# A ninth full set of block products in place of a half-depth one, plain merge gates, first block loads that the scheduler may place, and five background turns per tile of the first branch

## The chip, the cores and the metric

The kernel runs on one core of one Trainium2 chip. The metric is the device time of one execution in microseconds (us). Of the kernel before, three runs gave 1087.9, 1088.07 and 1090.32 us; the median is 1088.07. TensorE is called PE in the profile, VectorE DVE, ScalarE ACT, GpSimd POOL, SyncE SP; PEld is TensorE's loading of stationary operands.

## What is computed

One decoder layer in float32, for 256 tokens of width 2048:

```python
h = rmsnorm(x, pre_norm_g)
(a_q, a_k, a_v, a_g, a_lr, b_q, b_k, b_v, b_g, m_a, m_b) = split(h @ w_in)
o_a = rmsnorm(gla_chunked(a_q, a_k, a_v, gk(a_lr))) * silu(a_g)      # 4 heads
o_b = rmsnorm(diff_attention(b_q, b_k, b_v)) * (1 - lam_init) * silu(b_g)  # 16 heads
merged = sigmoid(m_a) * (o_a @ w_branch_a) + sigmoid(m_b) * (o_b @ w_branch_b)
out = x + rmsnorm(merged @ w_out, post_norm_g)
```

`w_in` has 2048 rows and some 18,000 columns; the other three matrices are 2048 by 2048. Nearly all the work is these products. `a_g`, the gate of the GLA branch (gated linear attention), and `m_a`, the merge gate of that branch, have 2048 columns each, which the kernel handles in four groups of 512: `ag0` to `ag3` and `m00` to `m03`.

## The kernel before, in words

**Precision.** Each float32 weight tile is split into a high part `hi` (ACT, line 362) and a rest `lo` (DVE, line 363), both in the fast format fp32r, and the activations are kept in two parts as well. A product takes three matmuls (hi by hi, hi by lo, lo by hi). The unit of the program is a *half tile*: 128 by 1024 weights, one `hi`, one `lo`. `take` hands out half tiles in the order of one list, `seq`, and prepares three of them ahead; `load` (L313) brings weights on SP's queue when a staging buffer is free.

**Plain tiles** (`token_major`). Both blocks of 128 tokens against 512 columns: eight half tiles of 12 matmuls, each 512 columns wide. **Channel tiles** (`half_channel`): 16 matmuls per half tile, the weights stationary, the result transposed.

**Sets** (`block_products`). A full set treats tokens, depth and 1024 weight columns as a 2 by 2 matrix of blocks and computes it with seven block products instead of eight, in the order `PRODUCTS`. A product has four half tiles (`t` and `h` are 0 or 1) of 6 matmuls each, so a set has 28 half tiles and 168 matmuls where two plain tiles have 16 and 192. The sums of weight blocks which the method needs are made by accumulating DMAs on POOL's queue (L256) and by DVE (L265), eight of these per set. Before, there are eight full sets (0 to 7) and a ninth, "quarter" one (`SETS` = 8) of half the depth: `ag3` and `m02` over half of the 2048 rows, 14 half tiles. The remaining halves of those two are plain tiles of four half tiles each (`QUARTER`); their sums with the quarter set's results are made by DVE on `rest` tiles fetched from DRAM. `ag0` and `ag1` are set 7; `ag2` is a plain tile of eight half tiles.

**Order in the set phase.** `phase_steps` writes it out: behind certain half products (`PARTNERED`) stands one half tile of other work, a *partner* (the last value group `v4`, the GLA keys and queries, the first two groups of differential queries and keys), 72 in all. A set takes eight, except at two slots named in `ALONE`; the first two products of set 0 take one more per slot (`front`).

**Behind the sets.** `ag2`, `ag3`, `m02`, then the query and key tiles of head groups 2 and 3, then `m03`; then the first branch, `y00` to `y03` (L1340 and on; of `y03` four half tiles), then the second branch and the output product. Beside them run background tasks, generators that do one step whenever a tile calls `pump`: first the scores of GLA (`gla_scores`, `pool.memset(suf)` on L960), then `gla_out`, which waits for four gates and so for `ag3`, and two lanes of differential attention (`diff_lane`). Behind `m03` the program pumps without other work until `gla_out` is done. In a plain tile `pump` is called after half tiles 1, 3, 5 and 7, otherwise `pump_eager`, which steps a task only if it said "go". A step of a lane: `scores` (matmuls L1134 to L1140, maxima on DVE, exponentials on ACT), `combine` (DVE, L1160), `turned` (three transposes on PE, L1165), `weighted` (L1176 to L1178; squares on ACT, a root on POOL, L465, then DVE, L1188), and per pair of heads `turned_out` (four transposes, L1194).

**Queues.** PE, ACT, DVE, POOL and SP each work through their instructions in the order that a scheduler has fixed; `keep_in_program_order` pins an instruction to its place in the program. DMAs of SP and POOL are issued by these two in that order too.

Of the kernel before, what the change touches and what calls it, by code (L numbers as in the profile page):

```python
# [14 lines left out]
P = 128  # L15
# [9 lines left out]
LANES = 3  # L25
X_LOADS = {0: (2, 2), 1: (4, 4), 2: (8, 4), 3: (12, 4)}
# [3 lines left out]
SETS = 8  # L30
GLA_GATES = 7
QUARTER = ("ag3", "m02")
MERGE = (0, 1, 6)
LEAD = 6
EARLY = (0, 1)
PARTNERED = ((1, 1), (3, 1), (5, 1), (6, 0), (6, 1), (2, 1), (7, 0), (7, 1))
SPILL_AT = (6, 0, 0)
LAST_PARTNERED = (1, 3, 5, 6, 2, 7)
ALONE = ((2, 6, 1), (5, 6, 1))
# [15 lines left out]
def chunk_plan():  # L55
# [16 lines left out]
    plan.append((f"set{GLA_GATES}", "set", "w_in", [(4096, 1024)]))  # L72
    plan.append((f"set{SETS}", "quarter", "w_in", [(5632, 512), (o + 9216, 512)]))
    for g in range(4):
        if g > 1:
            plan.append((f"ag{g}", "rest" if g == 3 else "tok", "w_in", [(4096 + 512 * g, 512)]))
# [3 lines left out]
        if g > 1:  # L80
            plan.append((f"m0{g}", "rest" if g == 2 else "tok", "w_in", [(o + 8192 + 512 * g, 512)]))
# [10 lines left out]
def tiles_of(n, kind):  # L92
# [3 lines left out]
    if kind == "quarter":  # L96
        return [(8 * i, 4, 512 * j, 512) for i in range(2) for j in range(2)]
    if kind == "rest":
        return [(r, 4, 0, n) for r in (4, 12)]
# [7 lines left out]
def phase_steps():  # L107

    keys = ["v4"] + [f"{name}{hf}{c}" for hf in range(2) for name in ("k", "q") for c in range(4)]
    keys += [f"{name}{g}{c}" for g in EARLY for pair in range(2) for name in ("dq", "dk") for c in (2 * pair, 2 * pair + 1)]  # L110
    other = [(key, r, h) for key in keys for r in range(4 if key == "v4" else 1) for h in range(2)]
    slots = [(s, prod, t) for s in range(SETS) for prod in PRODUCTS for t in range(2)]
    slots += [(SETS, prod, 0) for prod in PRODUCTS]
    front = [(0, prod, t) for prod in PRODUCTS[:2] for t in range(2)]
    mixed = []
    for slot in slots:
        mixed += [("set", *slot, h) for h in range(2)]
        s, prod, t = slot
        with_partner = prod in LAST_PARTNERED if s == SETS else (prod, t) in PARTNERED and slot not in ALONE
        for _ in range(with_partner + (slot in front)):  # L120
            mixed.append(other.pop(0))
# [29 lines left out]
def hybrid_kernel(ctx: ExitStack, tc, xt, xn, preg, postg, w, w2, gkb, glag, lamv, diffg, ident_d, causal_d, lmask_d, out):  # L151
# [60 lines left out]
    def heads_order(g):  # L212
        return halves_of(*(f"{name}{g}{c}" for pair in range(2) for name in ("dq", "dk") for c in (2 * pair, 2 * pair + 1)))

    seq = halves_of("v0", "v2", "v3") + phase_steps()
    seq += halves_of("ag2", "ag3", "m02") + heads_order(2) + heads_order(3) + halves_of("m03", *(f"y0{g}" for g in range(4)))[:-4]
# [10 lines left out]
    def block(s, i, t):  # L227
        return weights(f"set{s}", i if s == SETS else 2 * i + t)[0]

    def link(s, name, t):  # L230
        count[0] += 1
        c = blocks.tile([P, 2048], F32, tag="chain", name=f"{name}_{count[0]}", bufs=5)
        tc.keep_in_program_order((pool if s else sp).dma_start(c, block(s, {"a": 0, "b": 3}[name], t)))
        chain[s, name, t] = c

    def emit_set(s, prod, t, h):
        c = slice(1024 * h, 1024 * h + 1024)
        few = 1 if s == SETS else 2
        name, i = {(2, 0): ("a", 0), (7, 1): ("a", 1), (4, 0): ("b", 0), (4, 1): ("b", 1)}.get((prod, t), (None, 0))
        if h == 0 and s < SETS and name and (i == 0 or s + 1 < SETS):  # L240
            link(s + 1, name, i)
        if h == 0 and s == 0 and prod == 1:
            link(s, "b", t)
        n = 2 * few * (PRODUCTS.index(prod) - PRODUCTS.index(2)) + 2 * t + h + LEAD
        if 0 <= n < 2 * few:
# [6 lines left out]
    def follow_set(s, prod, t, h):  # L252
# [7 lines left out]
        steps = {(5, 0): 0, (2, 0): 0} if s == SETS else {(5, 1): 0, (6, 0): 1, (2, 1): 0, (7, 0): 1}  # L260
        i = steps.get((prod, t))
# [501 lines left out]
    gspill = [None] * (2 * SETS + 2)  # L763

    def merge_gate(banks, parts=None):
        t = u2([P, 2, 512], "mgate")
        for b in range(2):
            src = banks[b]
            if parts:
                src = parts[b]  # L770
                dve.tensor_tensor(out=src, in0=banks[b], in1=src, op=ALU.subtract)
            act.activation(t[:, b, :], src, AF.Tanh, scale=half_rstd[:, b : b + 1])
# [14 lines left out]
    def others():  # L787
# [24 lines left out]
        for g in EARLY:  # L812
# [879 lines left out]
```

## Time and profile before

| | |
|---|---|
| runs of the kernel before | 1087.9, 1088.07, 1090.32 us |
| the profiled execution's own time | 1087.73 us |
| its span in the profile | 1086.0 us |
| busy: PE, DVE, ACT, POOL | 1075.1, 939.7, 742.1, 164.0 us |
| matmuls recorded | 5416 |
| moved by DMA | 292.40 MB |

The span lies 1.73 us below the profiled execution's own time, and that lies 0.34 us below the median. A row of a timeline gives start, length, engine, line, operation, output and inputs, with the engine's idle time before it and who ended that in brackets; a length contains the pipeline, so the pace of PE is read from one start to the next. In a table by windows stands, per stretch, the busy time of each engine with its number of instructions, then PE's granted clock, the busy share of the DMA engines and GB/s.

### The profile page before, as it was taken

The page shows a single profiled execution, that of the slowest core. Times are in us where ns is not written, and L with a number is a line of the kernel's source. Part 1 is how long each engine was busy: PE and PEld are TensorE (multiplying, and loading weights), DVE is VectorE, ACT ScalarE, POOL GpSimd, SP SyncE. Part 2 cuts the span into 40 slices and gives each one's busy share as a digit, 9 for nine tenths or more (in the row PEclk, how much of TensorE's full clock was granted, in tenths as well). Part 3 has the DMA queues.
Part 4 walks back from the last instruction along what each step waited for, and adds up shares of the span by engine and source line. Part 5 has one row for each costly group of instructions (what it writes and reads, how often), then busy time and mean ns, then how long its engine had stood idle before and what let it go on. Part 6 is the DMA issues. An engine that isn't in the chain of part 4 may idle for free.

```text
span 1086.0 us, 15356 instructions
## 1 busy us (share of the span) xinstructions
PE 1075.1 (99%) x5416; PEld 920.2 (85%) x5416; DVE 939.7 (87%) x1276; ACT 742.1 (68%) x1068; POOL 164.0 (15%) x245
## 2 busy tenths in 40 slices
PE   9999999999999999999999999999999999999997
PEld 8999888888888888888888878888888888888886
DVE  7688989899998989899999799977778878889886
ACT  7886776767767677767676576566777776566662
POOL 0102112111201111222202110031011011100000
PEclk9999999999999999999999999999999999999999
DMA  8989998988989998999979766599897898988752
GB/s 320 291 299 323 272 299 218 344 175 344 218 289 249 327 265 252 298 261 320 210 273 256 282 209 221 195 330 317 271 301 257 276 295 275 322 296 260 272 191 98
DMA packets 66669, 292.40 MB, mean 269 GB/s; under 512 B 8672, under 2 KB 11744, under 8 KB 49184
## 3 DMA queue, kind: packets, MB, share of 16 engines
q1 hardware_dynamic: 38944, 177.43, 46.5%
q0 software_dynamic: 27072, 113.26, 38.6%
q8 instruction: 42, 0.69, 0.3%
q10 hardware_dynamic: 576, 0.73, 0.2%
q14 instruction: 35, 0.29, 0.1%
HBM read 264.12 MB, written 27.26 MB: 268 GB/s over the span
## 4 chain that ended last, share of the span: by engine, by line
PE 91%; DVE 3%; ACT 3%; issue 2%; DMA 1%; POOL 0%; POOLq 0%; SPq 0%; ACTq 0%; DVEq 0%
PE mm L559 58%; PE bg L559 23%; PE mm L547 2%; PE bg L547 2%; DMA raw<-in_w_dram 1%; DVE lo L363 1%; PE mm L532 1%; PE bg L998 1%; ACT hi L362 1%; PE bg L532 1%; PE bg L1165 0%; PE bg L1139 0%; PE bg L1140 0%; PE bg L1177 0%; PE bg L1178 0%
## 5 line engine op out<-in xcount | busy, mean ns | idle before, releaser
L362 ACT ACTIVATE hi<-raw 128x1024 fp32r<-128x1024 f32 (+3 forms) x237 | 242.7, 1029 | 155.2 <-PE mm L559 62.8
L363 DVE TENSOR_TENSOR lo<-raw,hi 128x1024 fp32r<-128x1024 f32 (+3 forms) x239 | 280.8, 1180 | 43.1 <-ACT hi L362 40.4
L559 PE MATMUL mm<-hi,xs 128*128 128x512 f32 (+1 forms) x728 | 185.3, 385 | 0.4 <-ACT hi L362 0.4
L362 ACT ACTIVATE hi<-a 128x1024 fp32r<-128x1024 f32 x136 | 144.0, 1061 | 52.0 <-PE mm L559 27.7
L363 DVE TENSOR_TENSOR lo<-a,hi 128x1024 fp32r<-128x1024 f32 x136 | 164.0, 1220 | 16.5 <-ACT hi L362 14.8
L559 PEld LDWEIGHTS mm<-hi,xs 128*128 128x128 f32 x728 | 134.9, 188 | 24.5 <-ACT hi L362 2.0
L559 PE MATMUL bg<-xs,hi 128*128 128x512 f32 x512 | 131.9, 389 | 0.0
L559 PEld LDWEIGHTS bg<-xs,hi 128*128 128x128 f32 x512 | 96.2, 188 | 18.7
L559 PE MATMUL mm<-lo,xs 128*128 128x512 f32 (+1 forms) x364 | 103.6, 384 | 0.8 <-DVE lo L363 0.8
L363 DVE TENSOR_TENSOR lo<-b,hi 128x1024 fp32r<-128x1024 f32 x68 | 82.5, 1220 | 15.8 <-ACT hi L362 14.0
L362 ACT ACTIVATE hi<-b 128x1024 fp32r<-128x1024 f32 x68 | 72.0, 1060 | 23.7 <-PE mm L559 15.6
L559 PEld LDWEIGHTS mm<-lo,xs 128*128 128x128 f32 x364 | 67.9, 188 | 14.1 <-DVE lo L363 2.3
L559 PEld LDWEIGHTS bg<-xs,lo 128*128 128x128 f32 x512 | 69.8, 190 | 5.0
L559 PE MATMUL bg<-xs,lo 128*128 128x256 f32 x512 | 71.4, 282 | 0.0
L559 PE MATMUL mm<-xs,hi 128*128 128x512 f32 x256 | 68.0, 397 | 0.0
L559 PEld LDWEIGHTS mm<-xs,hi 128*128 128x128 f32 x256 | 46.2, 189 | 7.8
L256 POOL DMA_DIRECT2D b<-in_w_dram x34 | 29.4, 866 | 150.8 <-DVE a L265 100.4
L559 PE MATMUL mm<-hi,oah 128*128 128x512 f32 x128 | 50.8, 397 | 0.0
L559 PE MATMUL mm<-hi,oal 128*128 128x512 f32 x128 | 50.0, 391 | 0.0
L362 ACT ACTIVATE hi<-c 128x1024 fp32r<-128x1024 f32 x34 | 36.1, 1061 | 14.3 <-PE mm L559 7.4
L265 DVE TENSOR_TENSOR a<-a,b 128x1024 f32<-128x1024 f32 x34 | 41.5, 1221 | 0.4
L265 DVE TENSOR_TENSOR a<-a,c 128x1024 f32<-128x1024 f32 x34 | 41.2, 1218 | 0.0
(419 smaller groups left out, 2174.9 us busy)
## 6 DMA issues: line engine op xcount, KB each, us to landing
raw<-in_w_dram SPq DMA_DIRECT2D x102, 1024.0 KB, 6.6
c<-in_w_dram SPq DMA_DIRECT2D x34, 512.0 KB, 9.1
a<-in_w_dram POOLq DMA_DIRECT2D x34, 512.0 KB, 9.5
b<-in_w_dram POOLq DMA_DIRECT2D x34, 512.0 KB, 6.2
a<-in_w_dram POOLq DMA_DIRECT2D x15, 1024.0 KB, 8.8
b<-in_w_dram POOLq DMA_DIRECT2D x15, 1024.0 KB, 9.0
raw<-in_w_dram SPq DMA_DIRECT2D x14, 832.0 KB, 6.4
gr<-gr POOLq DMA_DIRECT2D x9, 512.0 KB, 9.8
```

The source lines that it names most:

```text
L256: tc.keep_in_program_order(pool.dma_start(chain[s, name, i][:, c], block(s, 1, i)[:, c], accum_op=ALU.add))
L265: dve.tensor_tensor(out=a, in0=a, in1=chain[s, "b", i][:, c] if second else raws[s, i, h], op=ALU.add)
L362: act.activation(hi_t[:, a:b], r[:, a:b], AF.Copy)
L363: dve.tensor_tensor(out=lo_t[:, a:b], in0=r[:, a:b], in1=f32(hi_t[:, a:b]), op=ALU.subtract)
L532: i = pe.matmul(out, lhs, rhs, start=first and n == 0, stop=last and n == len(pairs) - 1, **kw)
L547: i = pe.matmul(banks[g][b][:, :n], a[part][:, P * b : P * b + P], w[:, n * g : n * g + n], start=first, stop=last)
L559: i = pe.matmul(*args, **kw)
L998: pe.matmul(o, xk[:, P * c : P * c + P], xq.rearrange("p (b c t) -> p b c t", b=2, c=4)[:, :, c, :], start=i == 0, stop=i == 1)
```

## The change

1. **Sets.** `SETS` is 9 and all are full. Sets 7 and 8 (`GLA_GATES`) are `ag0`, `ag1` and `ag2`, `ag3`. The quarter set, the plain tiles of `ag2` and `ag3` and the `rest` sums go. All four gates are fetched from DRAM before the GLA scores begin. `m02` becomes a plain tile of eight half tiles, its gate taken straight from PSUM.
2. **Partners.** Still 72. `front` is only the first product of set 0, and `ALONE` names slots of sets 4 and 8 instead of 2 and 5. Per set the numbers of partners go from 12, 8, 7, 8, 8, 7, 8, 8, 6 to 10, 8, 8, 8, 7, 8, 8, 8, 7. The last partner is now followed by four half products, before by two.
3. **First block loads.** The two `a` and two `b` loads of set 0, on SP, are no longer pinned.
4. **First branch.** In `y00` to `y03` the background gets its turns after half tiles 1, 2, 4, 5 and 7 (`BRISK`).
5. `EARLY` and the head groups are written by pairs, with the same order of work.

```diff
+BRISK = (1, 2, 4, 5, 7)
-SETS = 8
-GLA_GATES = 7
-QUARTER = ("ag3", "m02")
+SETS = 9
+GLA_GATES = (7, 8)
-ALONE = ((2, 6, 1), (5, 6, 1))
+ALONE = ((4, 6, 1), (8, 6, 1))
...
-    plan.append((f"set{GLA_GATES}", "set", "w_in", [(4096, 1024)]))
-    plan.append((f"set{SETS}", "quarter", "w_in", [(5632, 512), (o + 9216, 512)]))
+    for i, s in enumerate(GLA_GATES):
+        plan.append((f"set{s}", "set", "w_in", [(4096 + 1024 * i, 1024)]))
...
-    slots += [(SETS, prod, 0) for prod in PRODUCTS]
-    front = [(0, prod, t) for prod in PRODUCTS[:2] for t in range(2)]
+    front = [(0, PRODUCTS[0], t) for t in range(2)]
...
-        tc.keep_in_program_order((pool if s else sp).dma_start(c, block(s, {"a": 0, "b": 3}[name], t)))
+        i = (pool if s else sp).dma_start(c, block(s, {"a": 0, "b": 3}[name], t))
+        if s:
+            tc.keep_in_program_order(i)
...
-    def token_major(key, n, ops, step=1, upto=KT // 2):
+    def token_major(key, n, ops, step=1, upto=KT // 2, turns=(1, 3, 5, 7)):
         banks = [ps("mm"), ps("mm")]
-        for q in (2, 3, 6, 7) if key in QUARTER else range(upto):
-            half_tile(banks, n, q, ops, *take(key), begin=4 if key in QUARTER else 0)
-            if q % 2 or not ts:
+        for q in range(upto):
+            half_tile(banks, n, q, ops, *take(key))
+            if q in turns or not ts:
                 pump(step)
             else:
                 pump_eager()
...
-        if step == ("set", SETS, 2, 0, 0):
+        if step == ("set", SETS - 1, 7, 1, 0):
             fetched = [[fetch(ts[name, hf], name, u) for name in ("q", "k")] for hf in range(2)]
...
-    for g in range(2):
-        gates.append(fetch(gspill[2 * GLA_GATES + g], "ua", u2))
-    for g in (2, 3):
-        parts = other_parts(2 * SETS) if g == 3 else None
-        banks = token_major(f"ag{g}", 512, x_ops, LANES)
-        t = u2([P, 2, 512], "ua")
-        for b in range(2):
-            src = banks[b]
-            if parts:
-                src = parts[b]
-                dve.tensor_tensor(out=src, in0=banks[b], in1=src, op=ALU.add)
-            gate(src, b, t[:, b, :])
-        gates.append(t)
+    for n in range(4):
+        gates.append(fetch(gspill[2 * GLA_GATES[0] + n], "ua", u2))
...
-    parts = other_parts(2 * SETS + 1)
-    merge_gate(token_major("m02", 512, x_ops, LANES), parts)
+    merge_gate(token_major("m02", 512, x_ops, LANES))
...
-        banks = token_major(f"y0{g}", 512, a_ops, LANES, 4 if g == 3 else 8)
+        banks = token_major(f"y0{g}", 512, a_ops, LANES, 4 if g == 3 else 8, BRISK)
```

What moves, at the three places of which the prediction speaks. First SP's queue near the start, in the kernel before; `raw` are staging buffers of plain weights, `a` the first block of set 0, `w_raw` a small constant:

```order
25 L439 DMA lmask_504<-in_lmask_dram 128x256
26 L313 DMA raw_553<-in_w_dram 128x1664
27 L313 DMA raw_619<-in_w_dram 128x1664
28 L233 DMA a_679<-in_w_dram 128x2048
29 L233 DMA a_681<-in_w_dram 128x2048
```

The same block load on SP's queue in the changed kernel:

```order
11 L306 DMA raw_289<-in_w_dram 128x1664
12 L306 DMA raw_333<-in_w_dram 128x1664
13 L226 DMA a_679<-in_w_dram 128x2048
14 L306 DMA raw_377<-in_w_dram 128x1664
15 L422 DMA w_raw<-in_w_dram 16x1024 x4
```

One of the two `a` loads has moved forward by 15 rows, ahead of the last weights of the first tile and the constants; the other stays where it was.

Second, POOL at the end of the sets, in the kernel before; `dh` and `dl` are the spills of the last partner, `gr` and `gl` those of the last set, `ua` the fetched gates, `suf` a buffer of the GLA scores:

```order
126 L185 DMA dh_5458<-dh_5455 128x512
127 L185 DMA dl_5460<-dk_5283 128x512
128 L185 DMA gr_5485<-gr_5333 128x1024
129 L185 DMA gl_5487<-gl_5386 128x1024
130 L190 DMA ua_5497<-gl_5307 128x1024
131 L190 DMA ua_5499<-gr_5305 128x1024
132 L960 MEMSET suf_5537 128x1024
```

The same place on POOL in the changed kernel:

```order
128 L178 DMA dh_5594<-dh_5591 128x512
129 L178 DMA dl_5596<-dk_5381 128x512
130 L178 DMA gr_5643<-gr_5424 128x1024
131 L178 DMA gl_5645<-gl_5472 128x1024
132 L183 DMA ua_5655<-gl_5359 128x1024
133 L183 DMA ua_5657<-gr_5357 128x1024
134 L183 DMA ua_5659<-gl_5645 128x1024
135 L183 DMA ua_5661<-gr_5643 128x1024
136 L943 MEMSET suf_5699 128x1024
```

Between the spills and the memset stand four fetches instead of two, and the last two read what the two spills just ahead of them write.

Third, PE in the first branch, in the kernel before, from a `weighted` and a `turned` to the `turned_out` of the same pair; the rows left out are matmuls of the plain tile:

```order
2487 L1178 MATMUL bg_7687<-dv_7373,prob_631_7450 128x128
2488 L1165 MATMUL bg_7706<-ident,prob_644_7544 128x128 x3
2489 L559 MATMUL mm_7720<-hi_7584,oah_6601 128x512
...
2512 L559 MATMUL mm_7721<-lo_7654,oah_6603 128x512
2513 L1194 MATMUL mm_7756<-ident,ogb_7604 128x128 x4
2514 L1134 MATMUL bg_7786<-kl_6630,qh_6631 128x256
```

The same stretch on PE in the changed kernel:

```order
2396 L1161 MATMUL bg_7410<-dv_7158,prob_565_7204 128x128
2397 L1148 MATMUL bg_7429<-ident,prob_578_7283 128x128 x3
2398 L552 MATMUL mm_7232<-hi_7307,oah_6908 128x512
...
2409 L552 MATMUL mm_7233<-lo_7308,oah_6908 128x512
2410 L1177 MATMUL mm_7455<-ident,ogb_7327 128x128 x2
2411 L1117 MATMUL bg_7470<-kl_6832,qh_6833 128x256
2412 L1119 MATMUL bg_7470<-kh_6831,q_512_6830 128x128
2413 L1177 MATMUL mm_7455<-ident,ogb_7327 128x128 x2
```

Between `turned` and `turned_out` stood 24 matmuls of the tile; now it is 12 here, and `turned_out` is cut in two by the next scores. So it is at three of the eight `turned_out`; at the others it is still about 24.

More of the change, by code (lines that the diff above doesn't have):

```diff
@@ L95, in tiles_of @@
         return [(8 * i + 4 * t, 4, 512 * j, 512) for i in range(2) for j in range(2) for t in range(2)]
[L96 to L99, printed above, removed]
     if kind == "half":
@@ L118, in phase_steps @@
         s, prod, t = slot
-        with_partner = prod in LAST_PARTNERED if s == SETS else (prod, t) in PARTNERED and slot not in ALONE
+        with_partner = (prod, t) in PARTNERED and slot not in ALONE
         for _ in range(with_partner + (slot in front)):
@@ L210, in halves_of, with heads_order @@
         return [(key, r, h) for key in keys for r in range(len(at[key])) for h in range(2)]
-    def heads_order(g):
-        return halves_of(*(f"{name}{g}{c}" for pair in range(2) for name in ("dq", "dk") for c in (2 * pair, 2 * pair + 1)))
+    def heads_order(pairs):
+        return halves_of(*(f"{name}{g}{c}" for g, pair in pairs for name in ("dq", "dk") for c in (2 * pair, 2 * pair + 1)))
     seq = halves_of("v0", "v2", "v3") + phase_steps()
-    seq += halves_of("ag2", "ag3", "m02") + heads_order(2) + heads_order(3) + halves_of("m03", *(f"y0{g}" for g in range(4)))[:-4]
+    seq += halves_of("m02") + heads_order(PAIRS[EARLY:]) + halves_of("m03", *(f"y0{g}" for g in range(4)))[:-4]
     seq += branch_steps() + late_steps() + halves_of("o2", "o3")
@@ L227, in block @@
     def block(s, i, t):
-        return weights(f"set{s}", i if s == SETS else 2 * i + t)[0]
+        return weights(f"set{s}", 2 * i + t)[0]
     def link(s, name, t):
@@ L237, in emit_set @@
         c = slice(1024 * h, 1024 * h + 1024)
-        few = 1 if s == SETS else 2
         name, i = {(2, 0): ("a", 0), (7, 1): ("a", 1), (4, 0): ("b", 0), (4, 1): ("b", 1)}.get((prod, t), (None, 0))
-        if h == 0 and s < SETS and name and (i == 0 or s + 1 < SETS):
+        if h == 0 and name and s + 1 < SETS:
             link(s + 1, name, i)
@@ L867, in block_products @@
             out = bank[prod]
-            few = 1 if s == SETS else 2
-            for t in range(few):
+            for t in range(2):
                 for h in range(2):
@@ L879, in block_products @@
                                 first = prod not in ((6, 7, 2, 4) if seeded else (6, 7, 4)) and kt == 0 and w is hi and part == 0
-                                last = kt == 4 * few - 1 and w is lo
+                                last = kt == 7 and w is lo
                                 i = mm(out, a[part], w[:, 512 * j : 512 * j + 512], start=first, stop=last, skip_group_check=out is x or prod == 2)
                     latest[0] = i.ins
-                    if t == few - 1 and h:
+                    if t and h:
                         if prod == 1 and seeded:
@@ L910, in block_products @@
                             owed.append((2 * s, halves["l"], "gl"))
-                            if s == SETS:
+                            if s + 1 == SETS:
                                 settle_owed()
                     yield
-    sets = (step for s in range(SETS + 1) for step in block_products(s))
+    sets = (step for s in range(SETS) for step in block_products(s))
     rest = others()
```

81 lines of the change are left out of this document (33 added, 48 removed).

## The prediction

> **What bounds the kernel now.** I read the page first, its busy times and the chain that ended last:
>
> ```profile
> PE 1075.1 (99%) x5416; PEld 920.2 (85%) x5416; DVE 939.7 (87%) x1276; ACT 742.1 (68%) x1068; POOL 164.0 (15%) x245
> PE 91%; DVE 3%; ACT 3%; issue 2%; DMA 1%; POOL 0%; POOLq 0%; SPq 0%; ACTq 0%; DVEq 0%
> ```
>
> The chain runs through PE for 91% of the span. A busy PE need not be a PE at its pace, so the second view is the timeline of PE behind the sets, where plain tiles follow each other:
>
> ```profile
> 605.17 1.98 PE L559 MATMUL mm<-hi,xs 128*128 128x512 f32 x8
> 606.99 1.07 PE L559 MATMUL mm<-lo,xs 128*128 128x512 f32 x4
> 607.89 1.98 PE L559 MATMUL mm<-hi,xs 128*128 128x512 f32 x8
> ```
>
> A half tile of 12 matmuls goes from start to start in 607.89 - 605.17 = 2.72 us, 0.227 us each. Third, PE's waits by releaser:
>
> ```profile
> PE bg L991 <- DVE atl L977: 0.9, 1, 0.9
> ...
> PE mm L559 <- DVE lo L363: 0.8, 2, 0.4
> PE mm L559 <- ACT hi L362: 0.4, 1, 0.4
> ```
>
> Over the sets and tiles PE waits only 2.1 us. So PE's own matmuls are the time; what matters is how many there are and whether the other engines stay ahead. DVE is the nearest behind. Its load in the set phase, by windows that hold set 0, set 1 and set 2:
>
> ```profile
> 84.00:144.00 60.00, 60.00 (x296) 52.85 (x295) 55.77 (x58) 42.77 (x49) 9.91 (x14) 1.00 0.99 304
> 144.00:205.00 61.00, 61.00 (x301) 51.69 (x300) 55.84 (x56) 42.66 (x47) 10.78 (x15) 1.00 0.91 270
> 205.00:263.00 58.00, 57.59 (x280) 48.24 (x279) 52.21 (x50) 41.77 (x46) 10.67 (x15) 1.00 0.89 248
> ```
>
> DVE is busy 55.77 of 60, 55.84 of 61 and 52.21 of 58 us, so it has 4 to 6 us to spare in a set; ACT has far more. The granted clock is 1.00 throughout.
>
> **Part 1, matmuls.** Removed: the plain tile of `ag2` (8 half tiles of 12 matmuls = 96), the halves of `ag3` and `m02` (4 x 12 each = 96 together), the quarter set (14 half tiles of 6 = 84): 276. Added: a full set (28 x 6 = 168) and `m02` whole (96): 264. Twelve matmuls of 512 columns fewer, one half tile at the pace above: **-2.72 us**, all on PE's path.
>
> The Trainium skill, TensorE: Matmul & The Clock Gate, section "Back-to-back issue gap", gives about 131 ns per 512-column matmul in a sustained stream of loads and matmuls; by that the twelve would be worth 1.6 us, and the sum below 1.1 us smaller. The timeline here, with 227 ns from start to start, does not agree, and I go by the timeline.
>
> **Part 2, the engines beside PE in the sets.** A full set instead of the quarter set and the 16 plain half tiles is 36 half tiles (28 + 8) where there were 30 (14 + 8 + 4 + 4), 4 more block sums on DVE, and four `rest` sums fewer. The prices, from the groups of instructions on DVE:
>
> ```profile
> L363 DVE TENSOR_TENSOR lo<-a,hi 128x1024 fp32r<-128x1024 f32 x136 | 164.0, 1220 | 16.5 <-ACT hi L362 14.8
> L265 DVE TENSOR_TENSOR a<-a,b 128x1024 f32<-128x1024 f32 x34 | 41.5, 1221 | 0.4
> L972 DVE TENSOR_TENSOR xq<-xq,q 128x512 f32<-128x512 f32 x14 | 9.7, 690 | 4.3 <-DMA gr<-gr 4.3
> ```
>
> DVE gets (6 + 4) x 1.22 - 4 x 0.69 = +9.4 us (the last price is that of another 128x512 sum). The set phase grows with it: half a set more is 14 half tiles of about 1.4 us on PE. DVE stays near 92% there, so this costs nothing as long as partners lie between the half products. Where one is missing, this is PE in set 2, whose slot (6, 1) stands alone:
>
> ```profile
> 244.46 1.07 PE L559 MATMUL mm<-hi,xs 128*128 128x512 f32 x4
> 245.36 0.67 PE L559 MATMUL mm<-lo,xs 128*128 128x512 f32 x2
> 245.87 1.09 PE L559 MATMUL mm<-hi,xs 128*128 128x512 f32 x4
> 247.37 0.73 PE L559 MATMUL mm<-lo,xs 128*128 128x512 f32 x2 [0.41 <-DVE lo L363]
> ```
>
> Half a product takes 245.87 - 244.46 = 1.41 us, against 1.22 us of DVE for its `lo` alone; with block sums in between DVE falls behind, and PE waits 0.41 us. Of the two lone slots before, set 2 waited and set 5 did not. After, there are again two, in sets 4 and 8: 0, with 0.41 to either side. Set 0 loses two partners, two half tiles of 12 matmuls of 400 columns, some 4.5 us of PE cover, and with them about 2 us of DVE (both estimates from the two prices above). Its 4.2 us of idle DVE shrink to about 1.7. Still enough: 0 to +1 us, and I take **+0.3** for the unevenness. The 1 MB more of weights is 3.9 us of DMA at the 270 GB/s of the second window, spread over 520 us in which the DMA engines have about a tenth free: 0.
>
> **Part 3, the first block loads.** One 1 MB load moves from behind `raw_619` to ahead of the first tile's last weights. The windows at its new place and at its old one:
>
> ```profile
> 28.00:32.00 4.00, 4.00 (x23) 3.96 (x22) 3.29 (x6) 3.56 (x8) 0.00 (x0) 1.00 0.68 78
> 52.00:56.00 4.00, 3.62 (x20) 3.24 (x19) 2.98 (x6) 3.95 (x7) 0.00 (x0) 1.00 1.07 420
> ```
>
> It leaves a stretch at 420 GB/s for one that soon sinks to 78 GB/s. But PE's two waits near there are on ACT and on DVE:
>
> ```profile
> 54.29 1.02 PE L559 MATMUL mm<-hi,xs 128*128 128x416 f32 x4 [0.38 <-ACT hi L362]
> 78.69 0.65 PE L559 MATMUL mm<-lo,xs 128*128 128x416 f32 x2 [0.42 <-DVE lo L363]
> ```
>
> ACT is busy 3.95 of the 4 us around the first; an earlier DMA does not help it. The scheduler has also moved some conversions of this stage. I take 0, and 0.8 us to either side: both waits gone, or doubled. On SP the `a` load passes one `raw` of the first tile, the constants and four other `raw`, and one `b` load passes one `raw`; all of them have DMA time to spare there.
>
> **Part 4, from the sets to the GLA scores.** The first thing there is a wait for memory. PE, ACT and POOL in this order:
>
> ```profile
> 633.09 0.39 PE L990 MATMUL bg<-ath,ones_r 128*128 128x512 f32 x1
> 634.39 0.50 PE L991 MATMUL bg<-atl,ones_r 128*128 128x512 f32 x1 [0.92 <-DVE atl L977]
> 614.63 1.28 ACT L971 ACT_TABLE_LOAD   x1 [3.61 <-DMA dl<-dk]
> 608.78 0.55 POOL L185 DMA_DIRECT2D dl<-dk  x1 [0.52 <-DVE dk L784]
> 609.85 0.54 POOL L185 DMA_DIRECT2D gl<-gl  x1
> 610.91 0.54 POOL L190 DMA_DIRECT2D ua<-gr  x1
> 620.97 0.95 POOL L960 MEMSET suf<- 128x1024 f32 x1 [9.51 <-DVE att L956]
> gl<-gl POOLq DMA_DIRECT2D x9, 512.0 KB, 10.6
> ```
>
> ACT cannot start the scores until the last partner's spill has landed, 3.61 us of waiting, and the whole chain of the scores is late by that; 0.92 us of it reaches PE. After the change four half products follow the last partner instead of two, so the spill goes out 2 x 1.4 = 2.8 us earlier relative to the end of the sets. That covers 0.92 us: **-0.92**. Against it stands the new POOL order. POOL waits at the third fetch until set 8's spill has landed, and behind that fetch are the fourth, the memset of `suf`, and through it DVE's scores. With the median 10.6 us from 609.85 the spill lands at 620.5, and two issues of 0.54 put the memset at 621.5, 0.6 us later than now. But the spills of `gr` and `gl` stand behind that of the partner, and also move forward by up to 2.8 us, which makes it 618.7. So I keep -0.92, with +1 as the other end. The fetches of `q` and `k` come one product later and have some 10 us left; the gates are needed only behind the scores. Four ACT table loads go, with the Silu of `ag2` and `ag3`, on an engine that is 68% busy: 0.
>
> **Part 5, the background in the first branch.** Turns before `y00`: 28 before, 24 after; in `y00` to `y03` 14 before, 17 after. So the lanes start later and run denser. What PE finds at a `turned_out` now, in a tight and in a usual case, with DVE's L1188 that it needs:
>
> ```profile
> 857.79 0.49 PE L1165 MATMUL bg<-ident,prob 128*128 128x128 f32 x3
> 863.61 0.60 PE L1194 MATMUL mm<-ident,ogb 128*128 128x128 f32 x4
> 862.08 0.61 DVE L1188 SCALAR_TENSOR_TENSOR ogb<-bg,de,ub 128x128 f32<-128x128 f32 x2 [0.90 <-POOL de L465]
> 878.62 0.60 PE L1194 MATMUL mm<-ident,ogb 128*128 128x128 f32 x4
> 875.02 0.61 DVE L1188 SCALAR_TENSOR_TENSOR ogb<-bg,de,ub 128x128 f32<-128x128 f32 x2 [0.75 <-POOL de L465]
> ```
>
> DVE is done 863.61 - 862.69 = 0.92 us ahead in the tight case and 878.62 - 875.63 = 2.99 us in the usual one. At three of the eight places a half tile of 2.72 us goes out of that gap: a wait of 1.8 us in the tight case, none in the usual one. Bounds 0 to 5.4 us; I take **+0.7**, near the usual row. What hides the lanes' work elsewhere is the plain tile beside it.
>
> **The sum.** -2.72 + 0.3 + 0 - 0.92 + 0.7 = -2.64 us, so the profiled 1087.73 becomes 1085.1, and the median 1088.07 becomes **1085.4**. About 0.3%, 3.3 us, is what a measurement of this kernel can tell from no change: the limits are 1084.8 and 1091.3. The forecast lies just inside no change, and its own bounds reach over the lower limit.
>
> **The rivals.**
> *The waits go too.* Every PE wait of the sets and of the start (0.41 + 0.38 + 0.42) and the 0.92 disappear, and the lanes cost nothing: -2.72 - 2.13 = -4.85, 1083.2. For it: the partners are spread more evenly, and all waits are small. Against it: DVE's load does not fall.
> *DVE sets the pace, a little.* With nine full sets each one waits 0.41 us, as set 2 did: 8 x 0.41 = 3.3 above the forecast, 1088.7. Against it: only one of eight full sets waits now.
> *DVE sets the pace, wholly.* Then its 9.4 us count: 1097.5, slower. Against it: DVE idles 4 to 6 us per set. The Trainium skill, Perfetto Trace Analysis, section "Identifying the Most-Contended Engine", says matmul busy time misleads and LDWEIGHTS busy time should be read instead; by that rule PE at 85% stands behind DVE at 87%, and this rival would be the likeliest. Here PE's starts at a steady 0.227 us and its few waits speak against it.
> *POOL is late.* The memset holds the scores, +1 instead of -0.92: 1087.3.
> *The lanes stop PE.* PE works in order, so a transpose that comes too early stops the tile behind it. There are seven places where turns now follow after one half tile instead of two (two in each of `y00` to `y02`, one in `y03`). At 1.8 us each, the tight row everywhere: 12.6 us instead of 0.7, 1097.3, slower. It decides from about 6.6 us in all, 0.9 us per place. For it: the chain of a lane goes DVE, ACT, POOL, DVE. Against it: three of the seven are ahead of a `turned_out`, and usual slack is near 3 us.
>
> **How the numbers follow.** Chances: forecast 0.48, a third of that below 1084.8; the waits go too 0.25, all of it faster; DVE a little 0.09 and POOL late 0.09, both no change; the lanes 0.06 and DVE wholly 0.03, slower. Faster 0.16 + 0.25 = 0.41, same 0.32 + 0.18 = 0.50, slower 0.09. The range goes from 1082.6, the second case and 0.6 for what I have not seen, to 1088.8, DVE a little; what lies outside is the two slower cases and some of the edges, under 0.2.
>
> **What the profile after would show.** Matmuls fewer by 12, pace 0.227 us. PE's wait at the scores' `atl` row gone; if it has grown and POOL's memset stands later behind the `ua` fetches, part 4 is wrong. PE's waits on `lo` in sets 0, 4 and 8: none or one of 0.4. No PE wait at `turned_out` over 0.6 us; a list of waits there with DVE's L1188 or L1160 as releaser, several us in all, would make the forecast wrong, as would DVE rows named in every set.

## The result, and the profile after

The changed kernel takes 1102.15 us, the median of four runs from 1099.17 to 1103.47. Four runs of the kernel before beside them have a median of 1088.92, and the ratio is 1.0124, with a 95% interval from 1.0107 to 1.0141. It is slower by 13 us where a gain of 2.6 was forecast, and lies far above the range. Of two versions below, three runs took 1504 us or more, and the medians given there leave these out.

The profiled execution took 1099.17 us, its span is 1097.4 us. The page first, the lines that answer to the first two shown of before:

```profile
PE 1079.2 (98%) x5404; PEld 920.4 (84%) x5404; DVE 949.8 (87%) x1282; ACT 739.8 (67%) x1068; POOL 168.3 (15%) x249
...
PE 85%; DMA 8%; DVE 2%; issue 2%; ACT 2%; POOL 1%; POOLq 0%; SPq 0%; ACTq 0%; DVEq 0%
```

Twelve matmuls are gone, as forecast, and DVE is 10 us busier, as forecast (+9.4). What is new is in the chain: 8% of it, some 88 us, is now DMA, where it was 1%. Where that ends on PE is told by the waits, those of PE and the one on ACT behind the first of them:

```profile
ACT hi L355 <- DMA a<-in_w_dram: 25.0, 14, 3.4
...
PE mm L552 <- ACT hi L355: 7.3, 3, 2.5
...
PE mm L1177 <- DVE ogb L1171: 1.7, 2, 0.9
...
PE mm L552 <- DVE lo L356: 0.6, 1, 0.6
```

The wait at the GLA scores (`atl`) is gone and so are the two small ones at the start. But PE stops three times for about 2.4 us, each time for a `hi` that ACT could not make because the block `a` had not arrived. ACT waited 25.0 us for `a`; in the kernel before it was 2.3:

```profile
ACT hi L362 <- DMA a<-in_w_dram: 2.3, 2, 1.2
```

The three stops stand in sets 1, 2 and 4, at the fifth product, the one that reads `a` after block 1 has been added to it by the accumulating loads of L250. The chain through the first stop:

```profile
143.58 0.91 POOL a L250
...
146.90 18.12 DMA a<-in_w_dram
...
165.12 1.07 ACT hi L355
...
167.49 0.73 PE mm L552 x2
```

An accumulating load of 512 KB, issued at 146.90, lands 18.12 us later. To see why, POOL's queue in the timeline, here for set 2, from the first link of the next blocks (`a`, L226, 1 MB) to the four accumulating loads (L250):

```profile
176.02 0.55 POOL L226 DMA_DIRECT2D a<-in_w_dram  x1
195.58 0.53 POOL L178 DMA_DIRECT2D k<-k  x1 [19.02 <-DVE k L797]
196.13 0.54 POOL L226 DMA_DIRECT2D a<-in_w_dram  x1
196.92 0.54 POOL L226 DMA_DIRECT2D b<-in_w_dram  x1 [0.25 <-issue]
201.26 0.54 POOL L226 DMA_DIRECT2D b<-in_w_dram  x1 [3.79 <-DVE lo L356]
206.78 0.89 POOL L250 DMA_DIRECT2D a<-in_w_dram  x1 [4.98 <-DVE lo L356]
```

The same stretch of the kernel before:

```profile
185.58 0.53 POOL L185 DMA_DIRECT2D k<-k  x1 [5.17 <-DVE k L808]
186.10 0.55 POOL L233 DMA_DIRECT2D a<-in_w_dram  x1
195.80 0.55 POOL L233 DMA_DIRECT2D a<-in_w_dram  x1 [9.15 <-DVE lo L363]
200.88 0.54 POOL L233 DMA_DIRECT2D b<-in_w_dram  x1 [4.53 <-DVE lo L363]
206.02 0.54 POOL L233 DMA_DIRECT2D b<-in_w_dram  x1 [4.61 <-DVE lo L363]
211.54 0.89 POOL L256 DMA_DIRECT2D a<-in_w_dram  x1 [4.99 <-DVE lo L363]
```

Read the order, not the times alone. Before, the spill of `k` stood ahead of both `a` links; its wait of 5.17 us held up nothing that was needed soon, and the second `a` link left 211.54 - 195.80 = 15.7 us ahead of the accumulating loads. After, the spill stands *between* the two links. POOL works in order, so it sat 19.02 us on a `k` that was not yet made, with a link behind it that could have left some 5 us sooner: in a version below that takes the spill out of the way it leaves 15.5 us ahead of the accumulating loads (187.59 and 203.14). The second `a` link and the first `b` link then leave 0.8 us apart, only 10.7 us ahead of the accumulating loads. What that does to these is in the table of DMA issues, cut to the four accumulating loads of sets 1 to 5 of the changed kernel in turn (median us from issue to landing):

```profile
a<-in_w_dram POOLq DMA_DIRECT2D x4, 512.0 KB, 13.8
a<-in_w_dram POOLq DMA_DIRECT2D x4, 512.0 KB, 14.5
a<-in_w_dram POOLq DMA_DIRECT2D x4, 512.0 KB, 11.9
a<-in_w_dram POOLq DMA_DIRECT2D x4, 512.0 KB, 14.3
a<-in_w_dram POOLq DMA_DIRECT2D x4, 512.0 KB, 11.9
```

In the kernel before the same tables give 8.5, 8.7, 10.4, 10.2 and 8.8 us; this is its line for set 2:

```profile
a<-in_w_dram POOLq DMA_DIRECT2D x4, 512.0 KB, 8.7
```

The median alone does not tell where PE stops: in sets 6, 7 and 8 of the changed kernel it is 13.5, 14.0 and 13.7 us, and PE does not stop there. The last of the four loads does: it takes 18.1, 18.5 and 18.5 us in sets 1, 2 and 4, where PE stops, and 14.2 to 15.7 us in sets 3 and 5 to 8. PE's slack lies in between.

Why the spill moved: v4, k and q end when 8, 16, 24, 32 and 40 partners are done. Taking two partners out of set 0 makes each of these fall one or two partners later in its set. For v4 and the first k that changed the order on POOL: ahead of both `a` links before, between them now. The next q and k stood between the two links before as well, but were made early enough there; the link behind them then waited for its own buffer. For set 4, `k` waited 11.25 us in the kernel before and the link behind it 4.01 us more; in the changed kernel `k` waits 19.08 us, and the link goes out with no wait of its own. Now the spill is the later of the two. The last q went from between the `a` links to behind both, and no stop follows it.

A spill that waits between the links is not enough by itself. For set 3 of the changed kernel `q` waits 18.12 us there, and PE does not stop; for set 6 of the kernel before `dh` waits 18.89 us there, and the loads land in 10.6 us. The windows show one difference: ten us of the wait for `k` in the changed kernel, then of the wait for `dh` in the kernel before (the two figures at the end are the busy share of the DMA engines and GB/s).

```profile
186.78:196.78 10.00, 10.00 (x53) 8.56 (x53) 10.00 (x11) 6.21 (x8) 1.07 (x2) 1.00 0.40 141
428.54:438.54 10.00, 10.00 (x53) 8.55 (x53) 10.00 (x11) 6.80 (x9) 0.00 (x0) 1.00 0.87 320
```

While POOL waited for `k`, the DMA engines were busy for 0.40 of the time; while it waited for `dh`, SP's loads kept them at 0.87. In the 12 us from the first accumulating load on they are full in both (1.02 and 1.03), but SP moves 1.61 MB of that in the changed kernel and nothing in the kernel before. No run here changes SP's loads alone, so this part is read from the traces and not tested.

Behind the stops of sets 2 and 4 comes a second cost. PE's timeline in set 2:

```profile
230.40 0.79 PE L552 MATMUL mm<-hi,r1h 128*128 128x512 f32 x1 [2.38 <-ACT hi L355]
231.00 0.63 PE L552 MATMUL mm<-hi,r1l 128*128 128x512 f32 x1
231.42 0.63 PE L552 MATMUL mm<-hi,r1h 128*128 128x512 f32 x1
```

From start to start it is 0.43 us instead of 0.227, for some 3 us; the granted clock is 0.50 there. The last section comes back to this.

For a balance by stage I added up, over all matmuls of each trace, the time from one start to the next less the pace of its width (0.227 us for 512 columns, 0.189 for 416, 0.184 for 400, 0.120 for 256, 0.111 for 128). Stages are counted from the first matmul: the start to 100 us, the sets to 620, the GLA scores to 750, the first branch to 960, the rest.

| us above the pace | all matmuls at pace | start | sets | scores | first branch | rest |
|---|---|---|---|---|---|---|
| before | 1067.17 | 5.1 | 1.6 | 2.0 | 0.5 | 2.4 |
| changed | 1064.44 | 2.6 | 16.7 | 0.7 | 4.2 | 2.0 |

So the matmuls gained 2.7 us, the start 2.5, the scores 1.3; the sets lost 15.1 and the first branch 3.7. This is the balance of the two profiled executions, which lie 11.4 us apart (1087.73 and 1099.17 us); the medians lie 13.2 us apart.

### The profile page after: what moved, and what is told of

Its sections match the earlier page's. It is cut to its first block, busy times and chain, and to the rows that moved or that the text cites. A ratio compares the mean times of both kernels' runs of the same rounds, so it can differ in the third digit from the quotient of the medians.

```text
span 1097.4 us, 15374 instructions
## 1 busy us (share of the span) xinstructions
PE 1079.2 (98%) x5404; PEld 920.4 (84%) x5404; DVE 949.8 (87%) x1282; ACT 739.8 (67%) x1068; POOL 168.3 (15%) x249
## 4 chain that ended last, share of the span: by engine, by line
PE 85%; DMA 8%; DVE 2%; issue 2%; ACT 2%; POOL 1%; POOLq 0%; SPq 0%; ACTq 0%; DVEq 0%
PE mm L552 54%; PE bg L552 21%; DMA a<-in_w_dram 8%; PE mm L540 2%; PE bg L540 2%; DVE lo L356 1%; PE mm L525 1%; PE bg L981 1%; ACT hi L355 1%; PE bg L525 1%; POOL a L250 1%; ACT prob L1134 1%; DMA raw<-in_w_dram 0%; PE bg L1148 0%; PE mm L1177 0%
## 5 line engine op out<-in xcount | busy, mean ns | idle before, releaser
L355 ACT ACTIVATE hi<-raw 128x1024 fp32r<-128x1024 f32 (+3 forms) x229 | 234.2, 1028 | 147.7 <-PE mm L552 65.4
L356 DVE TENSOR_TENSOR lo<-raw,hi 128x1024 fp32r<-128x1024 f32 (+3 forms) x231 | 272.2, 1183 | 34.6 <-ACT hi L355 33.2
L356 DVE TENSOR_TENSOR lo<-a,hi 128x1024 fp32r<-128x1024 f32 x144 | 173.8, 1221 | 31.0 <-ACT hi L355 28.8
L355 ACT ACTIVATE hi<-a 128x1024 fp32r<-128x1024 f32 x144 | 151.4, 1058 | 70.3 <-DMA a<-in_w_dram 25.0
L552 PE MATMUL mm<-hi,xs 128*128 128x512 f32 (+1 forms) x688 | 175.2, 384 | 0.0
L552 PEld LDWEIGHTS mm<-hi,xs 128*128 128x128 f32 x688 | 128.2, 188 | 21.0
L356 DVE TENSOR_TENSOR lo<-b,hi 128x1024 fp32r<-128x1024 f32 x72 | 87.4, 1222 | 18.1 <-ACT hi L355 16.0
L552 PE MATMUL mm<-lo,xs 128*128 128x512 f32 (+1 forms) x344 | 99.0, 384 | 0.6 <-DVE lo L356 0.6
L355 ACT ACTIVATE hi<-b 128x1024 fp32r<-128x1024 f32 x72 | 76.4, 1061 | 29.5 <-PE mm L552 18.9
L552 PEld LDWEIGHTS mm<-lo,xs 128*128 128x128 f32 x344 | 64.0, 188 | 13.2 <-DVE lo L356 2.4
L250 POOL DMA_DIRECT2D b<-in_w_dram x36 | 30.9, 858 | 194.1 <-DVE a L258 88.8
## 6 DMA issues: line engine op xcount, KB each, us to landing
a<-in_w_dram POOLq DMA_DIRECT2D x36, 512.0 KB, 13.2
a<-in_w_dram POOLq DMA_DIRECT2D x16, 1024.0 KB, 10.4
```

The source lines that it names most:

```text
L250: tc.keep_in_program_order(pool.dma_start(chain[s, name, i][:, c], block(s, 1, i)[:, c], accum_op=ALU.add))
L355: act.activation(hi_t[:, a:b], r[:, a:b], AF.Copy)
L356: dve.tensor_tensor(out=lo_t[:, a:b], in0=r[:, a:b], in1=f32(hi_t[:, a:b]), op=ALU.subtract)
L552: i = pe.matmul(*args, **kw)
```

## The experiments

Three theories of the loss in the sets. **Q**, the queue: a spill that waits stands ahead of loads on POOL's queue, and these arrive late. **S**, the short set: set 0 lost two partners, half tiles of `k` with 8 matmuls of 512 and 8 of 256 columns each, 5.5 us at the pace; so the loads of set 1 and what follows have less time, whatever the spills do. **B**, the bytes: the ninth set's 1 MB, or the block loads at the start that are now placed otherwise.

### Twelve partners in set 0 again

```diff
-    front = [(0, PRODUCTS[0], t) for t in range(2)]
+    front = [(0, prod, t) for prod in PRODUCTS[:2] for t in range(2)]
-ALONE = ((4, 6, 1), (8, 6, 1))
+ALONE = ((2, 6, 1), (5, 6, 1), (8, 6, 1), (8, 7, 1))
```

> The ninth set, the plain merge gates, the unpinned loads and the five turns stay; only the partners of the first set are put back to 12, and two slots of the last set go without one. The background spills then stand on POOL's queue ahead of both first-half links of a set, as before. Theory Q (a spill that waits for its data stands between the two links on POOL's queue): no stop of PE over 1 us at the fifth product of sets 1, 2 and 4, the accumulating loads land in under 14 us, and the time falls by the three stops (7.9 us), the slow matmuls behind two of them (3 us) and the small ones, to 1087 to 1091 us. Theory S (set 0 itself is shorter by two partners, so all of set 1's loads have less time): the same 1087 to 1091 us. Theory B (1 MB more on the DMA engines and first loads that go out otherwise): 1100 to 1103 us, stops stay.

Measured: 1088.05 us, 0.9997 of before (0.9986 to 1.0007). The three stops are gone; set 2's accumulating loads land in 8.3 us. B falls: nothing of the ninth set or the first loads was touched. Q and S both stand. PE's largest waits are two others:

```profile
PE mm L1177 <- DVE ogb L1171: 2.4, 2, 1.7
PE mm L552 <- DVE gr L888: 1.8, 1, 1.8
```

The second is mine: it follows product 7 of the last set, where I had left two slots in a row without a partner.

### Only the spills moved on POOL's queue

The partners stay as in the changed kernel; the spills of v4, k and q are put on a list, which is emptied at product 4 of the set, behind the links (the edit for v4 reads alike).

```diff
-                                ts[name, hf] = spill(part, name)
+                                def put(key=(name, hf), t=part):
+                                    ts[key] = spill(t, key[0])
+                                held.append(put)
...
+                    if (prod, t, h) == (4, 0, 1):
+                        while held:
+                            held.pop(0)()
```

> The changed kernel with its ten partners in the first set; only on POOL's queue the spills of v4, k and q move behind the fourth link of the set, to a place where their data have long been made. Theory Q: stops gone, 1087 to 1091 us. Theory S (the set is too short for its loads): stops stay, 1100 to 1103 us. Theory B (bytes, first loads): stops stay, 1100 to 1103 us.

Measured: 1094.27 us, 1.0057 (1.004 to 1.0074), between the ranges of the theories. More than half of the loss is back: the stops of sets 2 and 4 are gone, but set 1 has two (1.26 and 1.72 us; the third wait, 0.79 us, is in set 6). PE's waits, then POOL's queue in set 1:

```profile
PE mm L552 <- ACT hi L355: 3.8, 3, 1.7
```

```profile
137.87 0.54 POOL L226 DMA_DIRECT2D b<-in_w_dram  x1 [3.66 <-DVE lo L356]
138.40 0.54 POOL L178 DMA_DIRECT2D vh<-vh  x1
138.93 0.54 POOL L178 DMA_DIRECT2D vl<-vl  x1
143.21 1.84 POOL L250 DMA_DIRECT2D a<-in_w_dram  x2 [3.75 <-DVE lo L356]
```

And the landing of set 1's accumulating loads:

```profile
a<-in_w_dram POOLq DMA_DIRECT2D x4, 512.0 KB, 15.4
```

No spill waits here any more, and the second `a` link leaves 4.9 us sooner than in the changed kernel (127.46 against 132.34). Yet these loads take 15.4 us, with the 1 MB of `vh` and `vl` issued just ahead of them. In set 2, with the 512 KB of `k` in that place, they land in 12.2 us, and PE does not stop. Either the spills' bytes count where they stand, or S holds for set 1.

### The spills behind the gate spills

The list is emptied at product 6 of the next set instead, with `gr` and `gl`.

> The changed kernel with the spills of v4, k and q held until the gate spills of the next set, behind the accumulating loads. With the spills just ahead of those loads, two stops of 1.4 and 1.9 us were left in set 1. Theory Q in its stricter form (whatever stands ahead of the accumulating loads, 1 MB of spill included): those two go as well, 1088 to 1091 us. Theory S (set 0 is 5.5 us shorter, so set 1's loads are late whatever the spills do): 2 to 4 us of stops stay at the fifth product of set 1 alone, 1091 to 1095 us.

Measured: 1113.68 us, 1.0243 (1.0229 to 1.0256), slower than the changed kernel, for a reason that neither theory had. PE's waits, then the row of DVE in set 1:

```profile
PE mm L552 <- DVE lo L356: 15.6, 5, 5.5
```

```profile
181.93 0.69 DVE L886 TENSOR_TENSOR gr<-mm,p 128x512 f32<-128x512 f32 x1 [5.16 <-DMA gl<-gl]
```

The held tiles and `gr` come from one pool of buffers. DVE stands 5.16 us at `gr` until a buffer is free, with the `lo` of the next half tiles queued behind it. But the question is answered in set 1, ahead of the first such wait: with ten partners in set 0 and no spill ahead of them, the accumulating loads land in 10.7 us, and PE does not stop at the fifth product of set 1. S falls there. The sets behind are shifted by the new waits and say nothing on this.

### The spills between the accumulating loads of `a` and `b`

The list is emptied at product 3 of the next set: late enough to be behind the loads that were late, early enough to give the buffers back.

```diff
-                    if (prod, t, h) == (4, 0, 1):
+                    if (prod, t, h) == (3, 0, 0):
```

> The changed kernel with its ten partners and its five turns; the spills of v4, k and q stand right behind the four accumulating loads of block 1 of the next set, ahead of those of b, so that nothing but the links is ahead of the loads that came late, and the data's buffers are held a third of a set less than behind the gate spills. Theory Q: no stop over 0.5 us at the fifth product of sets 1 to 4, no wait of DVE for a spilled buffer, 1086.5 to 1089.5 us. Theory S: 2 us or more of stops stay in set 1, 1090 to 1093 us. If holding the buffers costs here as it did behind the gate spills (waits of 2 to 6 us at the second product): 1095 us or more.

Measured: 1087.18 us, 0.9995 (0.9986 to 1.0004); the ratio to the changed kernel is 0.9995 / 1.0124 = 0.987. PE's waits, without those at the very ends, and set 1's accumulating loads:

```profile
PE mm L1185 <- DVE ogb L1179: 1.7, 2, 0.9
...
PE mm L552 <- DVE lo L356: 1.0, 2, 0.6
```

```profile
a<-in_w_dram POOLq DMA_DIRECT2D x4, 512.0 KB, 10.7
```

No stop at a fifth product, no wait for a buffer. The spills of five tiles moved on one queue, with everything else of the change in place, take back the whole loss.

### The kernel before with the partners of the changed one

```diff
-    front = [(0, prod, t) for prod in PRODUCTS[:2] for t in range(2)]
+    front = [(0, PRODUCTS[0], t) for t in range(2)]
-ALONE = ((2, 6, 1), (5, 6, 1))
+ALONE = ()
```

> The kernel before, with its half-depth ninth set, its pinned loads and its four turns; only the partners are those of the changed kernel (ten in the first set, and the two lone slots taken back), so that v4, k and q end between the two links of a set. Theories Q and S: the stops at the fifth product come without any other part of the change, two to four of 1.5 to 2.7 us with slow matmuls behind them, and the time is 1097 to 1105 us. Theory B (the ninth set's bytes, the first loads): no stop over 1 us, 1087.5 to 1090 us.

The partners are those of the changed kernel in sets 0 to 3, which hold four of the five spills; in sets 4 and 8 the counts differ by one. Measured: 1101.88 us, 1.0138 (1.012 to 1.0156), as slow as the changed kernel. Its waits and POOL's rows of set 2:

```profile
PE mm L559 <- ACT hi L362: 9.4, 6, 3.0
```

```profile
178.66 0.54 POOL L233 DMA_DIRECT2D a<-in_w_dram  x1
198.13 0.53 POOL L185 DMA_DIRECT2D k<-k  x1 [18.93 <-DVE k L808]
198.68 0.55 POOL L233 DMA_DIRECT2D a<-in_w_dram  x1
```

Set 2's accumulating loads land in 15.0 us; three stops of 2.36 to 2.95 us stand in sets 1, 2 and 4. The balance differs from that of before almost in the sets alone: 16.8 us instead of 1.6 there, and under 1 us in any other stage. The shift of the partners makes the loss by itself, without the ninth set, the first loads or the turns.

### The first loads pinned again

```diff
-        if s:
-            tc.keep_in_program_order(i)
+        tc.keep_in_program_order(i)
```

> The changed kernel with the four first loads of set 0 pinned in the order of the program again. Theory B in its form that these loads displace others: 1088 to 1092 us and no stops. Theories Q and S: the stops stay, 1100 to 1103 us, within 1 us of the changed kernel.

Measured: 1107.03 us, 1.018 (1.016 to 1.02), 5 us above the changed kernel, where Q and S had allowed 1 us. B in this form is wrong in its sign: the start goes from 2.6 to 4.9 us above the pace, so the free loads are a gain of 2.3 us. In the sets the stops grow from 16.7 to 21.2 us and come in set 3 too, where the accumulating loads land in 12.5 us instead of 11.9 (the last of them in 17.2 instead of 14.8). The first branch goes from 4.2 to 7.7 us above the pace as well. Why the sets and the first branch shift with the start stays open.

### Four turns again, and six

```diff
-        banks = token_major(f"y0{g}", 512, a_ops, LANES, 4 if g == 3 else 8, BRISK)
+        banks = token_major(f"y0{g}", 512, a_ops, LANES, 4 if g == 3 else 8)
```

> The changed kernel with four background turns in eight half tiles of the first branch, as before. All theories of the stops: those stay. If the lanes cost what the changed kernel's trace shows at the turned tiles (about 2 us of waits of PE that were not there before), 1099.5 to 1101 us; if those waits only replace others, within 0.5 us of the changed kernel.

Measured: 1113.85 us, 1.0244 (1.0223 to 1.0265), 12 us more than the changed kernel: a miss. The first branch goes from 4.2 to 15.8 us above the pace. Its largest stop in PE's timeline:

```profile
946.00 1.38 PE L1177 MATMUL mm<-ident,ogb 128*128 128x128 f32 x4 [2.06 <-DVE ogb L1171]
```

Without the plain tiles of `ag2` and `ag3` the lanes have 24 turns ahead of the first branch instead of 28. With four turns per tile the last pairs are done where hardly a tile is left to cover them; in PE's order the transposes of the last pair stand directly behind its weighted sums, with no half tile between. With the ninth set in place the fifth turn is needed; it is not an extra.

To see what the turns cost by themselves, the kernel before with five of them (the same list of turns in the first branch, nothing else):

> The kernel before with one edit: five background turns (1, 2, 4, 5, 7) in eight half tiles of the first branch. In the order of PE two pairs' transposes then stand one half tile behind their weighted sums. If the distance is what costs: stops of 0.8 to 1.8 us at two or three places, and 1089 to 1092 us; if it is the missing tiles of the ninth set's partners that made the lanes late, no stop, 1087 to 1088.5 us.

Measured: 1091.53 us, 1.0046 (1.0033 to 1.006). The first branch goes from 0.5 to 5.7 us above the pace; the largest of its stops:

```profile
898.01 0.33 PE L1194 MATMUL mm<-ident,ogb 128*128 128x128 f32 x1 [1.76 <-DVE ogb L1188]
```

In PE's order the transposes of four of the eight pairs now stand one half tile behind their sums (my expectation had counted two). The time lies in its first range, that of a distance which costs; the spread turns below put a limit on that reading.

### Towards a faster one

Twelve partners in set 0, and the two lone slots that this needs in the last two sets, one in each: `ALONE = ((2, 6, 1), (5, 6, 1), (7, 6, 1), (8, 6, 1))`.

> As the version with twelve partners in the first set, whose 1.99 us stop stood behind the seventh product of the last set, where two slots in a row were without a partner; here the two lone slots lie in the last two sets, one in each, at the sixth product. If that stop came from the missing partner: it goes, 1085.5 to 1087.5 us, 1 to 3 us below the kernel before. If it is the wait for the sum of the right half whatever stands beside it: 1088 to 1089 us.

Measured: 1087.02 us, 0.9999 (0.9989 to 1.0009); the stop behind product 7 is gone, the time is still that of before. What is left are 5.3 us in the first branch. Then the turns at other half tiles, first six (`BRISK = (1, 2, 3, 4, 5, 7)`), then five spread otherwise (`BRISK = (1, 2, 3, 5, 7)`):

> As the one before it in this call, with six background turns in eight half tiles of the first branch instead of five. If the stops of 0.9 and 1.8 us at the turned tiles come from lanes that run late, they shrink, and the time falls by 0.5 to 2 us against five turns; if they come from lanes too close to their own producers, they grow by as much.

> The version with twelve partners and one lone slot in each of the last two sets, with the five background turns at half tiles 1, 2, 3, 5 and 7 instead of 1, 2, 4, 5 and 7. In the order of PE the transposes of a finished pair then stand two or three half tiles behind the weighted sums that they need in every case; with the other list they stood one half tile behind at three of eight places, and PE stopped 0.91 and 1.38 us at two of them. If that distance is the cause: these stops go, the time falls by 2 to 2.5 us, to 1084 to 1086 us, and this beats both kernels. If the lanes are late for another reason (more turns in the same tiles): stops of the same size stay, 1086.5 to 1088 us.

Six turns: 1093.67 us, 1.0054 (1.004 to 1.0068). The first branch stands 10.5 us above the pace; the denser turns bring the transposes of six of the eight pairs to one half tile or less behind their sums. Five turns spread: 1085.36 us, 0.9983 (0.9972 to 0.9993), by the ratio 1.8 us below before, and the only kernel here whose interval lies below 1. It is not settled that the turns did it. The transposes wait 0.4 us now instead of 2.1, but another wait of 1.3 us took their place, and the profiled executions, 1086.91 us with the first list and 1087.64 with this one, show no gain. By the balance the first branch stands 5.4 us above the pace with this list and 5.3 with the first, although all eight `turned_out` are again 24 or more matmuls behind their sums, as in the kernel before, where it was 0.5. So the distance decides at which transposes PE stops; it is not shown to be what five turns cost:

```profile
PE bg L1148 <- DVE ogb L1171: 1.3, 2, 1.1
...
PE mm L1177 <- DVE ogb L1171: 0.4, 1, 0.4
```

Last, this list of turns in the version with the spills held until product 3 (this version is "the one before it" here):

> As the one before it in this call, with the background turns at half tiles 1, 2, 3, 5 and 7. If both edits do what they did alone: 1.5 to 2.5 us below it, 1084.5 to 1087.5 us, level with the fastest version so far or just below it; if the buffers are held too long, both are slow alike.

Measured: 1087.42 us, 1.0 (0.9989 to 1.001), no better than with the old list; the first branch stands 5.6 us above the pace instead of 4.2. So the spread turns gave nothing there, and 1.8 us is the most that any version here has shown.

## Why the prediction was wrong, point by point

**The step that failed** is in part 2: "this costs nothing as long as partners lie between the half products", with "0 to +1 us" for the two partners that set 0 loses. I weighed a partner as matmuls that cover PE and as work that loads DVE. A partner also issues DMAs, and the last of each group puts a spill on POOL's queue, ahead of whatever stands there. Moving the partners made each of these spills the thing for which the next link on POOL waits, and the sets lost 15.1 us, of which 12.7 come back when the spills alone move (16.7 to 4.0 us above the pace). POOL's order before and after could have shown it, and the row of `k` in the timeline of before was a spill that waited; I did not ask what such a wait costs when it is moved. The "0" for the DMA engines failed in the same place: their mean share said nothing about when one load is due, and while POOL waited for `k` in the changed kernel it was 0.40. The two lost partners themselves were sized wrongly too: they are half tiles of `k`, 5.5 us in all, not of v4, 4.5.

**Part 1** held: 1067.17 less 1064.44 is 2.73 us for -2.72.

**Part 2, DVE** was too low by 2 us. With the spills out of the way (the version that puts them at product 3) the sets stand 4.0 us above the pace, 2.4 more than before, for +0.3. Two waits for `lo`, 1.0 us in all, are part of it, the rest is in intervals under 0.3 us each; there is no list of waits on DVE in every set.

**Part 3** was undersized: a gain of 2.5 us for 0, outside the 0.8 to either side, and 2.3 of it is lost again when the loads are pinned. Both small waits went, 1.1 us from start to start, and as much again in intervals of under 0.14 us.

**Part 4** held: the wait at `atl` is gone, 1.3 us for 0.92, and the memset did not hold the scores.

**Part 5** was undersized: 3.7 us for +0.7, inside its bounds of 0 to 5.4. Two transposes wait, 0.8 and 0.9 us, each about half of the tight row's 1.8; the rest is in small pieces, for which the sum had no term. The usual row, no wait, was the wrong one to lean on. I had not asked what four turns would cost here: 12 us.

Without the failed step, in the version with the spills at product 3, the balance is -2.7 at the pace, -2.9 in the start, +2.4 in the sets, -1.1 at the scores, +3.7 in the first branch and -0.5 in the rest, together -1.1 us from the first matmul to the last; its ratio, 0.9995, says -0.5. So the forecast would have been 1.5 to 2 us too low even then: the gain of the ninth set is spent in the first branch and in the sets.

None of the rivals had the mechanism. Two of them ended slower, the lanes at 1097.3 us and DVE wholly at 1097.5; either would have had the sign right by accident. DVE wholly is ruled out: with the spills at product 3 DVE is busy 947.9 us, 8.2 more than before, and the time is 0.9995 of before.

## What to carry to other kernels

A piece of work that is moved takes all its instructions along: list the queues that it issues on, and for each ask what it will stand in front of, and whether it will be waiting there. On a queue that works in order, a store that waits for its data belongs behind the loads that wait for nothing, but not so far behind that its buffer is missed. A mean share of DMA says whether the bytes fit, not whether one load is in time; that is read from its landing against the moment it is needed.

## What I had not expected of the hardware

**A short stop can cost twice.** A stop of 2.38 us was followed by matmuls at 0.43 us instead of 0.227 for some 3 us, 1.5 us in all; a longer one in set 1 (2.51 us) was followed by none. The Trainium skill, TensorE: Matmul & The Clock Gate, section "HAM oscillation — how this bites in real kernels", gives the rule as no PE-idle gaps above some 3.4 us. As to the length this trace does not agree: stops under 2.6 us lowered the clock in two cases of three. What tells the cases apart is in the record of the granted clock. In the changed kernel the clock is at 0.50 for two stretches behind the stops, each 3.41 us long; they begin at 229.96 and 356.26 us, 126.30 us apart, which is 37 times 3.413. With the first loads pinned there are four, at 169.50, 234.36, 299.21 and 364.06 us, 64.85 apart, 19 times 3.413. So in these traces the clock changes on a grid of 3.41 us. On this grid, the two stretches that the stop of set 1 touches, then the one of set 2's stop and the one behind it (PE's busy time is the figure behind the comma, the clock the third from the end):

```profile
161.70:165.11 3.41, 2.02 (x9) 1.33 (x8) 1.39 (x2) 0.07 (x1) 0.76 (x1) 1.00 1.06 303
165.11:168.52 3.41, 2.24 (x8) 1.54 (x9) 2.31 (x3) 3.40 (x4) 0.00 (x0) 1.00 1.06 211
226.55:229.96 3.41, 1.41 (x5) 0.49 (x4) 1.02 (x2) 0.66 (x1) 0.00 (x0) 1.00 1.05 261
229.96:233.37 3.41, 2.97 (x7) 2.39 (x8) 2.99 (x3) 3.14 (x4) 0.00 (x0) 0.50 0.82 163
```

The stop of set 1 lies across a line of the grid, with 1.39 us of idle PE on one side and 1.17 on the other; that of set 2 puts 2.00 us into one stretch. Over all the traces here, from 11 to 1078 us, the stretch just ahead of each fall of the clock holds 1.62 us of idle PE or more, and no stretch that is followed by a full clock holds more than 1.76. Where a stop falls counts beside its length.

**Landing time moves with what stands ahead on the queue.** The same four 512 KB accumulating loads of set 2, with ten partners in set 0, landed in 10.5 us with the spill of `k` behind them, 12.2 with it just ahead of them, 14.5 with it holding up a link; with twelve partners and the spill ahead of all links it was 8.3. PE stopped only at 14.5. It is not the queue alone: for set 6 of the kernel before a spill holds up a link for as long, and the loads land in 10.6 us.
